# Entry of layer 0's feed-forward: token sums and spread inside the first plain half panel, the third sum ahead of the scaling, the two plain panels in turn

## The chip, the core and the metric

The kernel runs on one core of a Trainium2 chip. The metric is the device time of the whole program, in microseconds (us). The core's engines each take their own instructions in the order in which they were laid down: TensorE (PE) multiplies into PSUM, with its weight loads (PEld) beside it; VectorE (DVE) and ScalarE (ACT) do the elementwise work; GpSimdE (POOL) and SyncE (SP) mostly issue DMAs here.

## The reference, cut to what matters

Two layers of a hybrid backbone over 512 latent tokens and 256 context tokens, 1024 features. The stage around the change is the feed-forward of layer 0, in fp32:

```python
h_lat = h_lat + g_a * o_lat                       # attention's output projection
h_lat = h_lat + g_f * swiglu(modulate(h_lat, sh_f, sc_f), ffn_w_gate_up[l], ffn_w_down[l])
# the same for h_ctx with the context modulation
def rms_norm(x): return x * lax.rsqrt(jnp.mean(x * x, axis=-1, keepdims=True) + EPS)
def modulate(x, shift, scale): return rms_norm(x) * (1 + scale) + shift
def swiglu(h, w_gate_up, w_down):
    g, u = jnp.split(h @ w_gate_up, 2, axis=-1)
    return (jax.nn.silu(g) * u) @ w_down
```

Before the first gate-up product can run, a token's 1024 features must all have their residual, be squared and summed, and the token's features be scaled by the inverse root.

## The kernel before, in words

Features lie on the 128 partitions in 8 tiles (k = 0 to 7), tokens along the free axis: 768 for layer 0, in two halves of 384, TOK1 and TOK2. Every fp32 product is made from three matmuls: each operand is split into a rounded high part (a cast on ACT) and a low part (a subtraction on DVE), and high x high, high x low and low x high are added in PSUM. `parts` (line 1288), `split` (line 340) and `load_w` (line 301) make such splits; `three` (line 757) and `product` (line 1297) issue the matmuls.

`output` (line 1186) makes the attention's output projection with the residual, tile by tile, first for TOK2 and then for TOK1, and beside the TOK1 tiles it normalises TOK2. `Norm.add` squares a residual tile on ACT and adds it to a running sum on DVE (line 355). `Norm.rest` then calls `rstd`: token sums as matmuls with a column of ones (line 365), root on ACT (366), reciprocal on DVE (367), and `spread` (line 449), three transposes of the broadcast column that put the token factors into a PSUM bank. After that `use` of `combined` (line 1246) scales each tile on DVE (line 1235), adds the shift on ACT (line 1236) and splits it. For TOK2 the scaled tiles are called far, for TOK1 near.

The feed-forward's 22 gate-up column blocks (128 columns of the gate and 128 of the up matrix each) come in two kinds. In layer 0 block 0 is done plainly: two panels, gate and up, by the two token halves, four half panels of 24 matmuls (`half` in `first_pairs`). Blocks 1 to 21 are each a `Pair` (line 1306): a scheme with 7 products instead of 8 over the two halves of the features and of the columns, for which sums of the operands are needed: T1 to T4 from the far and near tiles (`sums`, line 1267) and s1 to s4 from the weights (`Pair.weights`, lines 1313 to 1333). Of a pair, `head` needs near operands alone, `body` needs T2, T3 and T1, `tail` needs T4. The head's bank z is copied out (line 1341) before the body adds T2's product to it. The tail of a pair comes after the head of the next.

Modulation vectors still to be made are background steps: `bg(n)` runs n of them. Here two steps of layer 0's last component remain (matmuls of line 191, whose weights lie in the buffers ph and pl, and line 195), then tiles of layer 1 (two DVE products of line 215 each, with the weights in the single buffer rope0).

The order on each engine is set by a planner: it simulates the program and gives an engine the ready instruction that stands first in the code; a buffer is taken when its first writer is placed. `in_order(engine)` (line 630) fixes the order of the instructions in its block on that engine. Buffers that matter: p has 8, ph and pl 4 each, PSUM tags s, t, o, d have 3, 2, 1, 2.

## Time and profile before

| | us |
|---|---|
| median of 3 runs (1613.65, 1618.28, 1618.03) | 1618.03 |
| the profiled execution's own time | 1612.09 |
| its span | 1610.3 |
| PE busy in the span | 1539.6 (96%) |
| DVE busy | 1182.0 (73%) |
| ACT busy | 806.0 (50%) |
| mean granted TensorE clock | 0.986 |

Times inside the profile count from the span's start. A row of the timeline gives start, length, engine, line, operation, output<-inputs, shape and count; in brackets stands how long the engine was idle before it and what ended that. Successive matmuls and elementwise instructions overlap a little, so the cost of one in a row of many is the distance from start to start. A matmul on plain fp32 data (token sums, modulation) is recorded as two passes.

### The profile page before, as it was taken

The numbers are of one execution on the slowest core, as the hardware profiler recorded it, in microseconds if no ns is written. First come the engines' busy times: TensorE is split into PE (matmuls) and PEld (weight loads), VectorE is DVE, ScalarE is ACT, GpSimd is POOL, SyncE is SP. The second block draws the span as 40 slices with busy tenths as digits, with TensorE's granted clock in tenths as the row PEclk, the third lists the DMA queues.
The fourth block names the chain that finished last, engine by engine and source line by source line (L and its number), as shares of the span: only waits on it lengthen the run. The fifth ranks groups of instructions, "written<-read, shape, count | busy, mean of one in ns | idle before, by whom it ended". The sixth has DMA issues, their size and how long they took to land.

```text
span 1610.3 us, 26632 instructions
## 1 busy us (share of the span) xinstructions
PE 1539.6 (96%) x10004; PEld 1375.9 (85%) x10004; DVE 1182.0 (73%) x2367; ACT 806.0 (50%) x1637; POOL 226.7 (14%) x219
## 2 busy tenths in 40 slices
PE   6999989999998999999999998999999999999997
PEld 4686877887988999998989997877889898899996
DVE  5495977577579687785867776768877688687686
ACT  5364587776455333342423244457756554454453
POOL 0152723230000000100000010283003000000000
PEclk9999999999998999999999999999999999999998
DMA  9445342004541465647565766121006133333322
GB/s 341 161 149 190 108 132 80 23 7 159 179 161 59 158 204 169 214 127 246 159 202 196 243 212 210 41 89 66 2 6 200 33 112 124 91 98 118 91 97 84
DMA packets 80465, 214.92 MB, mean 133 GB/s; under 512 B 10192, under 2 KB 17872, under 8 KB 80336
## 3 DMA queue, kind: packets, MB, share of 16 engines
q1 hardware_dynamic: 73552, 188.05, 36.5%
q0 software_dynamic: 4480, 22.02, 3.7%
q10 hardware_dynamic: 2304, 3.15, 0.5%
q8 instruction: 78, 1.28, 0.3%
q14 instruction: 51, 0.42, 0.1%
HBM read 186.97 MB, written 23.07 MB: 130 GB/s over the span
## 4 chain that ended last, share of the span: by engine, by line
PE 73%; DVE 12%; DMA 9%; issue 3%; ACT 2%; POOL 1%; SPq 0%; DVEq 0%; ACTq 0%
PE pso L532 5%; DMA rope<-in_mod_w_dram 4%; PE pss L320 4%; PE pss L321 4%; PE pss L322 4%; PE psd L320 3%; PE psd L321 3%; PE psd L322 3%; PE pss L1302 3%; PE pss L1304 3%; PE pss L1303 3%; PE psd L1304 3%; PE psd L1302 3%; PE psd L1303 3%; PE pst L479 2%
## 5 line engine op out<-in xcount | busy, mean ns | idle before, releaser
L307 ACT CAST wh<-wr 128x512 fp32r<-128x512 f32 (+2 forms) x142 | 108.4, 778 | 202.9 <-PE pss L321 43.3
L308 DVE TENSOR_TENSOR wl<-wr,wh 128x1024 fp32r<-128x1024 f32 (+2 forms) x139 | 127.1, 921 | 78.6 <-ACT wh L307 77.9
L538 ACT ACTIVATE p<-p,sm 128x512 f32<-128x512 f32 (+3 forms) x144 | 105.0, 730 | 26.3 <-DVE sm L542 24.0
L215 DVE CUSTOM_DVE_ANT_0 p<-rope,cond 128x1024 bf16<-128x1024 f32 x64 | 77.0, 1220 | 40.3 <-DMA rope<-in_mod_w_dram 40.1
L321 PE MATMUL psd<-b,wh 128*128 128x256 f32 (+4 forms) x257 | 87.7, 341 | 2.2 <-DVE b L1290 2.2
L1303 PE MATMUL pss<-b,wh 128*128 128x384 f32 (+1 forms) x270 | 84.0, 311 | 1.2 <-DVE b L345 1.2
L1302 PE MATMUL pss<-b,wh 128*128 128x384 f32 (+1 forms) x270 | 84.1, 311 | 0.7 <-ACT b L344 0.7
L1430 POOL DMA_DIRECT2D home<-p x40 | 21.6, 541 | 447.5 <-DVE p L1166 320.5
L1304 PE MATMUL pss<-b,wl 128*128 128x384 f32 (+1 forms) x270 | 83.9, 311 | 0.0
L320 PE MATMUL psd<-b,wh 128*128 128x512 f32 (+4 forms) x217 | 77.8, 358 | 2.1 <-ACT b L430 1.3
L320 PE MATMUL pss<-st,wh 128*128 128x256 f32 (+2 forms) x231 | 78.1, 339 | 0.4 <-ACT wh L307 0.4
L322 PE MATMUL pss<-st,wl 128*128 128x512 f32 (+2 forms) x231 | 77.8, 337 | 0.0
L532 PE MATMUL pso<-ph,b 128*64 128x256 f32 (+1 forms) x384 | 77.3, 359 | 0.3 <-DVE ph L470 0.2
L532 PE MATMUL pso<-pl,b 128*64 128x256 f32 (+1 forms) x384 | 76.8, 359 | 0.7 <-DVE pl L470 0.7
L322 PE MATMUL psd<-b,wl 128*128 128x512 f32 (+4 forms) x217 | 76.0, 351 | 0.0
L1304 PE MATMUL pst<-b,wl 128*128 128x384 f32 (+1 forms) x240 | 74.1, 310 | 0.6 <-DVE wl L1290 0.6
L1302 PE MATMUL pst<-b,wh 128*128 128x384 f32 (+1 forms) x240 | 74.5, 310 | 0.0
L1303 PE MATMUL pst<-b,wh 128*128 128x384 f32 (+1 forms) x240 | 74.5, 310 | 0.0
L321 PE MATMUL pss<-b,wh 128*128 128x256 f32 (+4 forms) x227 | 74.0, 327 | 0.1
L1289 ACT CAST wh<-ph 128x512 fp32r<-128x512 f32 x80 | 46.3, 620 | 43.8 <-PE pst L1303 14.6
L1302 PE MATMUL psd<-b,wh 128*128 128x384 f32 (+1 forms) x210 | 65.8, 313 | 0.0
L1304 PE MATMUL psd<-b,wl 128*128 128x384 f32 (+1 forms) x210 | 65.3, 313 | 0.5 <-DVE wl L1290 0.5
(606 smaller groups left out, 5385.0 us busy)
## 6 DMA issues: line engine op xcount, KB each, us to landing
wr<-in_w_gu_dram SPq DMA_DIRECT2D x88, 512.0 KB, 4.1
rope<-in_mod_w_dram SPq DMA_DIRECT2D x48, 512.0 KB, 3.5
wr<-in_w_out_dram SPq DMA_DIRECT2D x32, 512.0 KB, 3.6
wr<-in_w_dn_dram SPq DMA_DIRECT2D x64, 256.0 KB, 2.8
p<-home SPq DMA_DIRECT2D x40, 384.0 KB, 4.8
home<-p POOLq DMA_DIRECT2D x40, 384.0 KB, 4.5
wr<-in_w_in_dram SPq DMA_DIRECT2D x21, 512.0 KB, 4.0
st<-in_mod_wp_dram SPq DMA_DIRECT2D x32, 256.0 KB, 4.9
```

What stands on the lines that cost most here:

```text
L215: V.tensor_tensor_reduce(out=T("p", [P, D], mybir.dt.bfloat16), in0=w, in1=cond[:, v, :], op0=ALU.mult, op1=ALU.add, scale=1.0, scalar=0.0 ...
L307: S.copy(h, r)
L308: (G if eng else V).tensor_tensor(lo, r, f(h), op=ALU.subtract)
L320: PE.matmul(o, wh[:, k], mh[:, c], start=first and k == 0, stop=False)
L321: PE.matmul(o, wh[:, k], ml[:, c], start=False, stop=False)
L322: PE.matmul(o, wl[:, k], mh[:, c], start=False, stop=last and k == n - 1)
L532: ins = PE.matmul(o[64 * i : 64 * i + 64, c], v(kt), t, start=n == 0, stop=n == len(moving[i]) - 1)
L538: S.activation(p[:, c], p[:, c], AF.Exp, bias=nm, scale=-1.0, accum_out=dn)
L1289: S.copy(h, t)
L1302: PE.matmul(o, wh, xh, start=first and k == 0, stop=False, skip_group_check=not first)
L1303: PE.matmul(o, wh, xl, start=False, stop=False, skip_group_check=not first)
L1304: PE.matmul(o, wl, xh, start=False, stop=k == 3, skip_group_check=not first)
```

## The change

1. `output` gets `hold`. In layer 0's second stream (TOK1) the last tile's square is kept as a second tile, `norm.last`, instead of being added to the running sum, and the normalisation is not run there.
2. `first_pairs` for layer 0: the far half of panel 0 is begun with four of its eight feature tiles (12 matmuls); then the token sums over the two square tiles, root and reciprocal; then `third`, which makes T3 = far's second half minus its first and splits it; then the other 12 matmuls, the spread, and the far half of panel 1. PE's order is fixed over all that.
3. Then the scaling of TOK1 (`norm.use`), and the near halves of both panels in turn, in a fixed order on PE: for each pair of feature tiles the products with the high part of both panels, then the products with the low part of the pair before.
4. `sums` makes T1 and T2 (and T3 in layer 1, where the operands are narrow) of all four tiles first, then T4 in place in the near tiles.
5. The two background steps that stood between the far and near halves are run after the head of pair 1, those after the head of pair 1 after that of pair 2.
6. `token_sums`, `inverse` and `spread_to` are moved or named; the end of layer 0 uses them as before.

```diff
-                norm.add(m, c)
+                if hold and i and m == KT - 1:
+                    norm.last = square_sum(None, norm.src[m], c)
+                else:
+                    norm.add(m, c)
...
+            if hold and i:
+                return
...
+    def token_sums(d, accs, n):
+
+        for i in range(n // P):
+            for j, a in enumerate(accs):
+                PE.matmul(d[:, i : i + 1], a[:, i * P : (i + 1) * P], ones[:, :1], start=j == 0, stop=j == len(accs) - 1)
...
+    def spread_to(col, n):
+
+        o = PS("o")
+        spread(o, [col[:, i : i + 1].to_broadcast([P, P]) for i in range(n // P)])
+        return o
...
+            xs = []
             for i in range(4):
                 tag = "st" if i < 2 else "b"
-                x, y = B(tag="p"), B(tag="p")
...
+                x = B(tag="p")
+                xs.append(x)
...
-                several(x, ("T1", "T2"), tag)
-                V.tensor_tensor(y[:, at1], b22, b12, op=ALU.subtract)
-                V.tensor_tensor(y[:, at2], b21, x[:, at2], op=ALU.subtract)
-                several(y, ("T3", "T4"), tag)
+                several(x, ("T1", "T2", "T3") if narrow else ("T1", "T2"), tag)
+            for i, x in enumerate(xs):
+                tag = "st" if i < 2 else "b"
+                y = near[i][:, at2]
+                V.tensor_tensor(y, y, x[:, at2], op=ALU.subtract)
+                ops["T4"].append(parts(y, *(spare[i] if narrow else (unit(tag), unit(tag)))))
+
+        def third():
+
+            for i in range(4):
+                x = B(tag="p")[:, at1]
+                V.tensor_tensor(x, far[i][:, at2], far[i][:, at1], op=ALU.subtract)
+                ops["T3"].append(parts(x, *(unit("st" if i < 2 else "b") for _ in range(2))))
...
+        if l == 0:
+            with in_order(ON_PE):
+                o = begun(0, 1, order[:4])
+                d = PG()
+                token_sums(d, (norm.acc, norm.last), HT)
+                col = inverse(d, HT)
+                V.reciprocal(col, col)
+                third()
+                begun(0, 1, order[4:], o)
+                r = Columns(spread_to(col, HT), 0)
+                ended(0, 1, o)
+                half(1, 1)
+            for k in order:
+                norm.use(k, r, cs[0], 0)
+            near = [PG()[:, : cs[0].stop] for _ in range(2)]
+            with in_order(ON_PE):
+                for i in range(5):
+                    for o, (h, lo) in zip(near, (ws[0], ws[1])):
+                        for k in (i, i + 4) if i < 4 else ():
+                            x = ops[("11", "21")[k // 4]][i][0]
+                            PE.matmul(o, h[:, k], x, start=k == 0, stop=False)
+                            PE.matmul(o, lo[:, k], x, start=False, stop=False)
+                    for o, (h, _) in zip(near, (ws[0], ws[1])):
+                        for k in (i - 1, i + 3) if i else ():
+                            PE.matmul(o, h[:, k], ops[("11", "21")[k // 4]][i - 1][1], start=False, stop=k == 7)
+            for n in range(2):
+                ended(n, 0, near[n])
+            return [x for x, _ in tiles]
...
-        if l == 0:
-            bg(2)
...
-                    if l == 0 and j == DIRECT[0]:
+                    if l == 0 and j < 3:
                         bg(2)
```

`begun` issues a half panel's matmuls for the feature tiles it is given, `ended` applies Silu or the product with the other panel and splits the result; together they are the former `half`.

More of the change, by code (lines that the diff above doesn't have):

```diff
@@ L1367, in first_pairs, with begun @@
         ws = {}
-        def half(n, second):
+        order = (0, 4, 1, 5, 2, 6, 3, 7)
+        def begun(n, second, ks=order, o=None):
             j, i = panels[n]
@@ L1433, in hybrid_kernel @@
     first_w, banks3 = [], []
-    def token_sums(d, accs, n):
-        for i in range(n // P):
-            for j, a in enumerate(accs):
-                PE.matmul(d[:, i : i + 1], a[:, i * P : (i + 1) * P], ones[:, :1], start=j == 0, stop=j == len(accs) - 1)
-    def inverse(d, n):
-        col = T("sm", [P, 6, 2])[:, : n // P, 0]
-        S.activation(col, d[:, : n // P], AF.Sqrt, bias=eps, scale=1.0 / D)
-        return col
     def final0(src, hs):
```

37 lines of the change are left out of this document (21 added, 16 removed).

## The prediction

> **What bounds the kernel now.** I read the busy time by stage first. Its columns are the stretch, its length, the busy time of PE, PEld, DVE, ACT and POOL with instruction counts, then granted clock, DMA share and GB/s.
>
> ```profile
> 466.78:513.10 46.32, 38.54 (x208) 34.61 (x208) 39.24 (x68) 24.05 (x40) 0.54 (x1) 0.85 0.17 55
> 477.50:487.20 9.70, 4.39 (x30) 2.71 (x29) 8.54 (x20) 8.99 (x17) 0.00 (x0) 0.75 0.21 56
> 487.20:492.70 5.50, 5.49 (x17) 5.49 (x18) 5.50 (x9) 2.58 (x4) 0.00 (x0) 0.51 0.00 0
> 505.60:513.10 7.50, 5.04 (x17) 4.23 (x16) 7.33 (x12) 1.74 (x3) 0.00 (x0) 0.77 0.24 85
> 513.10:560.00 46.90, 46.65 (x266) 44.66 (x266) 30.36 (x54) 17.55 (x34) 0.16 (x1) 1.00 0.45 144
> 560.00:700.00 140.00, 140.00 (x802) 133.21 (x801) 112.31 (x193) 49.80 (x89) 8.49 (x16) 1.00 0.58 189
> 800.00:1003.00 203.00, 193.54 (x1070) 180.79 (x1068) 143.48 (x247) 71.03 (x133) 12.98 (x24) 0.99 0.63 209
> ```
>
> The stretch from 466.78 (first matmul of layer 0's feed-forward) to 513.10 (last product of the body of pair 1) is the only one near the change in which PE is not full: 46.32 - 38.54 = 7.8 us idle, at a mean clock of 0.85. Behind it PE is full for hundreds of us, so a gain won here should reach the end.
>
> Then the order of instructions in that stretch, PE first:
>
> ```profile
> 466.78 0.33 PE L758 MATMUL psd<-st,wh 128*128 128x384 f32 x1
> 470.78 0.33 PE L760 MATMUL psd<-b,wl 128*128 128x384 f32 x1
> 471.04 0.41 PE L191 MATMUL pst<-ph,cond_col 128*32 128x256 f32 x2
> 472.45 0.83 PE L365 MATMUL pss<-ones,p 128*128 128x1 f32 x6
> 473.15 0.42 PE L758 MATMUL pss<-st,wh 128*128 128x384 f32 x1
> 477.26 0.33 PE L760 MATMUL pss<-b,wl 128*128 128x384 f32 x1
> 478.09 0.54 PE L449 MATMUL pso<-ident_r,sm 128*128 128x128 f32 x3
> 483.93 0.69 PE L758 MATMUL pss<-b,wh 128*128 128x384 f32 x1 [1.96 <-ACT b L344]
> 487.21 0.69 PE L759 MATMUL pss<-b,wh 128*128 128x384 f32 x1 [1.64 <-DVE b L345]
> 509.36 0.44 PE L1302 MATMUL pss<-st,wh 128*128 128x384 f32 x1 [0.57 <-ACT p L1348]
> 512.48 0.52 PE L1303 MATMUL pss<-b,wh 128*128 128x384 f32 x1
> 512.80 0.47 PE L1304 MATMUL pss<-b,wl 128*128 128x384 f32 x1
> ```
>
> A plain half is 24 matmuls of 0.174 us ((470.78 - 466.78)/23). The token sums run only at 472.45, behind the first half and modulation matmuls, and the column is spread only at 478.09, behind the second half. DVE waits for exactly that:
>
> ```profile
> 467.89 1.23 DVE L1290 TENSOR_TENSOR wl<-wr,wh 128x1024 fp32r<-128x1024 f32 x1 [0.29 <-ACT wh L1289]
> 469.03 0.55 DVE L355 TENSOR_TENSOR p<-p,p 128x384 f32<-128x384 f32 x1
> 471.75 0.69 DVE L1323 TENSOR_TENSOR pl<-wr 128x512 f32<-128x512 f32 x1 [2.17 <-PE pst L191]
> 474.29 0.17 DVE L367 RECIPROCAL sm<-sm 128x3 f32<-128x3 f32 x1
> 478.66 4.29 DVE L1235 SCALAR_TENSOR_TENSOR p<-b,mod,pso 128x384 f32<-128x384 f32 x8 [4.21 <-PE pso L449]
> 506.02 1.21 DVE L215 CUSTOM_DVE_ANT_0 p<-rope,cond 128x1024 bf16<-128x1024 f32 x1
> 507.16 0.95 DVE L345 TENSOR_TENSOR b<-p,b 128x768 fp32r<-128x768 f32 x1
> 516.79 1.23 DVE L215 CUSTOM_DVE_ANT_0 p<-rope,cond 128x1024 bf16<-128x1024 f32 x1 [3.86 <-DMA rope<-in_mod_w_dram]
> ```
>
> DVE idles 2.17 and 4.21 us and then runs from 478.66 without a gap. The last low part of a T operand ends at 508.11; PE ends the pair's body 5.0 us behind it. In the chain of waits (start, length, what) DVE carries it throughout; one each of a scaling, a subtraction and a 768-wide low part, the length being the time to the next start:
>
> ```profile
> 478.66 0.20 DVE p L1235
> 485.22 0.47 DVE p L1282
> 507.23 0.87 DVE b L345
> ```
>
> So from 478.66 on **DVE sets the end of this stage**; before, the spread's place in PE's order does.
>
> **The change part by part.** First, the token sums. They now come after 12 of the first half's 24 matmuls: 466.78 + 12 x 0.174 = 468.87. Six passes took 473.15 - 472.45 = 0.70 us; with two tiles instead of one they are twelve, 1.4 us, end 470.3. The second tile is the square of the last residual, which ACT has ready in time:
>
> ```profile
> 467.76 0.52 ACT L352 ACTIVATE p<-b 128x384 f32<-128x384 f32 x1
> 473.32 0.26 ACT L366 ACTIVATE sm<-pss,eps 128x3 f32<-128x3 f32 x1 [5.05 <-PE pss L365]
> 478.18 0.62 ACT L1289 CAST ph<-wr 128x512 fp32r<-128x512 f32 x1 [4.59 <-PE psd L191]
> 478.81 1.28 ACT L1378 ACT_TABLE_LOAD   x1
> 480.11 0.49 ACT L1378 ACTIVATE p<-psd 128x384 f32<-128x384 f32 x1
> 481.01 2.14 ACT L1236 ACTIVATE p<-p,mod 128x384 f32<-128x384 f32 x4
> 483.05 0.83 ACT L344 CAST b<-p 128x768 fp32r<-128x768 f32 x1
> 500.86 0.47 ACT L1341 COPY p<-pss 128x384 f32<-128x384 f32 x1
> ```
>
> 467.76 + 0.52 = 468.28, 0.6 us ahead of its use; the DVE addition at 469.03 falls away. Root (0.26) and reciprocal (0.17) with some 0.3 us of hand-over end at 471.0; the other 12 matmuls cover that until 472.4. If the cover went (DVE busy with up to three third sums ahead of the reciprocal) each would cost 0.47 us, and the slack of 1.4 us takes three. The spread (0.5 us) then ends at 472.9: **DVE's scaling starts 478.66 - 472.9 = 5.8 us earlier.**
>
> Second, the third sums move ahead of the scaling. Before, each was a subtraction of 0.47 us and half of a 768-wide low part (T3 and T4 shared it; half of 0.87), inside DVE's closed block: 4 x 0.90 = 3.6 us. Now they are 4 x (0.47 + 0.47) = 3.8 us (384-wide low part, nearest row the 384-wide operations), in the 3.4 us between 469.5 and 472.9 that hold nothing urgent. What leaves the block is 3.6 less an overhang of 0.4: **-3.2 us**. Their four casts ride on ACT, which before sat 5.05 us and then 4.59 us idle there: nothing, as long as the root comes first.
>
> Third, four weight sums of pair 1 (471.75 to 474.3, 4 x 0.6) used that gap before. The third sums take it now, and the modulation matmuls that hold the ph and pl buffers move behind the head of pair 1, so these sums slide into the block: **+2.4 us**. The bounds are 0 (PE runs those matmuls in any idle moment, being ready) and 2.4; I take the upper, since the gap is full.
>
> Fourth, the steps of background modulation move one pair later. The matmuls of line 191 cost PE the same wherever they stand. The two layer-1 tiles (line 215) follow pair 2's head instead of pair 1's, and the first of their four products stood in the block at 506.02: **-1.1 us** if it leaves, 0 if it stays; I take -1.1, since every instruction of pair 2's weights now goes ahead of it.
>
> Fifth, the near halves run in turn and in a fixed order. Per index PE needs 12 x 0.174 = 2.1 us, DVE two scalings of 0.54 and a low part of 0.87 = 1.95, ACT two Identities of 0.53 and a cast of 0.72 to 0.83 = 1.8 to 1.9. PE is the slowest by a little; the second far half (24 x 0.174 = 4.2) keeps it at work until 477.1, while ACT gives the first high parts at 472.4 + 1.28 + 0.49 + 2 x 0.53 + 0.83 = 476.1. So the run starts without a wait and costs nothing by itself. But the lead is 1 us, and other casts and sums share both engines' queues, which run in order: I put **+1.0** on DVE's block for waits on ACT, between 0 and 2.3 (a third cast or two in between each time).
>
> Sixth, T4 goes behind all the other sums: the same DVE work, ahead of pair 1's weights either way: 0, and up to -3.6 if it goes behind them.
>
> The sum for the last operand of pair 1's body: -5.8 - 3.2 + 2.4 - 1.1 + 1.0 = -6.7, so 508.1 becomes 501.4. PE runs out of near and head matmuls at about 477.1 + 8.4 + 4.2 = 489.7, or 492 with the modulation matmuls, and then takes T operands as they come. It will be cold again as it was at 509.36 (12 matmuls, 0.32 us apart, in 512.80 + 0.32 - 509.36 = 3.8 us instead of 2.1), so I leave the 5.0 us between last operand and last product as they are: 506.4 instead of 513.1. Of that, DVE's earlier end is kept for the following pairs, since PE is 99% full from there. **Gain 6.7 us.** In the profiled execution (span 1610.3, its own time 1612.09) that is 1605.4; against the median of the runs, 1618.03, **1611.3**. The profiled execution lies 6 us under that median, as the fastest run (1613.65) lies 4 us under it, so chance among runs is as large as what I look for.
>
> One rule speaks on the cold clock. By the Trainium skill, page "TensorE: Matmul & The Clock Gate", section "HAM oscillation — how this bites in real kernels", PE drops to half clock only when it idles more than about 3.4 us. Here the clock fell to half at 509.36 after waits of which none was over 1.2 us (7.50 - 5.04 = 2.5 us in all within that stretch), and by 487.2 after waits under 2 us: the trace does not bear the rule out as a limit for single gaps. By the rule the new body would run at full clock after short gaps, which would give some 1.7 us more (1609.6, an estimate); the sum keeps the trace's price.
>
> **The rivals.** *PE becomes the bound.* With all of DVE's deferrable work (T4, the layer-1 products, next pair's sums) behind the operands, PE sees no gap: 46.32 us less 7.8 idle, less the half-clock loss (17 matmuls at 487.2, four from 483.93 and 12 at 509.36, each 0.32 - 0.174 = 0.146: 4.8), plus 0.7 for the doubled token sums: 34.4 us, end 501.2, gain 11.9, **1606.1**. For it: the rows per index above balance, and PE has 12 us of loss to give. Against it: DVE's continuous work.
>
> *The queue takes it back.* The layer-1 products keep their place, and because the first now runs earlier than the second tile can be loaded, DVE waits for the DMA in front of pair 1's remaining weights as it did at 516.79: 6.7 - 1.1 - 3.86 = 1.7 gained, **1616.3**. For it: that wait stood in the chain already, after a product which had been ready long before. Against it: these products now rank behind pair 2's weights.
>
> *The change loses: p buffers.* Eight exist. The four near tiles now live until T4 and the four x tiles too, so pair 1's s and t get none until T4 begins, and the copy of z (line 1341, at 500.86 before) must precede T2, T3 and T1. If T4 stands last: operands 501.4, T4's first part 0.94 + a cast 0.5, copy 0.5, body 36 matmuls (the first 12 cold: 3.8 + 4.2) and 0.6 for the second copy: 511.9, no gain; and if the two layer-1 products and their DMA wait stand ahead of T4 too (1.1 + 1.1 + 3.9): 518.0, **1622.9**. It decides once z's copy comes later than about 504. For it: the count of tiles. Against it: nothing else of DVE's is as urgent by then, and T4 ranks before the weights.
>
> That the change doesn't do what it says is open only for the order outside the two fixed runs, where a planner decides again, also for the chunk boundaries behind 800 (203.0 - 193.54 = 9.5 us of idle PE, which may move by a few us either way).
>
> **How the numbers follow.** A measurement of this kernel can tell about 0.3%, 4.9 us, from no change. Forecast 0.47, with a range of its own of 1608 to 1615; PE-bound 0.23; taken back 0.22; p buffers 0.08. Of the forecast's 0.47 I count 0.05 as under 4.9 us. Faster is 0.42 + 0.23 = 0.65, same 0.05 + 0.22 = 0.27, slower 0.08. The range reaches from 1605 (PE-bound, with a us for chance) to 1617 (taken back, likewise), and leaves out the last rival.
>
> **What would show it.** The 12-pass token sums before 470.5 and a spread near 472.5; first scaling near 473; the four third sums ahead of it; near matmuls at 0.174 us from about 477, without waits over 1 us; the layer-1 products after 510; the body's last product of pair 1 near 506. It would be wrong if ACT's first high parts came after 478 (the fixed run then stands still and goes cold), if DVE shows gaps over 2 us before 500, if z's copy of pair 1 comes after 504, or if the stretch ends earlier and the chunk boundaries behind it lose the same.

## The result, and the profile after

The changed kernel takes 1607.57 us (median of 5 runs, 1605.55 to 1609.28), the kernel before 1618.03 in the runs beside it. The ratio is 0.9942, with a 95% interval of 0.9927 to 0.9957: 9.4 us gained by the ratio, 10.5 by the medians. Measured a second time beside other runs of the kernel before, it came to 0.9936 (0.9919 to 0.9952). The forecast was 6.7 us gained and 1611.3; the range of 1605 to 1617 holds the time, which lies 0.4 us under the 1608 to 1615 that the forecast had by itself.

The profiled execution of the changed kernel has a span of 1603.8 us. In it PE comes to layer 0's feed-forward at 468.29, and before at 466.78, although PE's order and its idle time ahead of it (29.9 us) are the same; over the profiles of this document that moment lies between 466.75 and 471.22. So 1.5 us are chance among executions, and I measure from the first far matmul of the stage. I call the stretch from there to the first residual addition of the down projection *the stage*; it holds the same work in both kernels but for six more passes of token sums. The windows of it, first before, then after (columns as in the prediction: stretch, length, then busy time of PE, PEld, DVE, ACT, POOL, and clock, DMA share, GB/s):

```profile
466.78:557.16 90.38, 82.35 (x459) 76.92 (x459) 67.14 (x118) 40.20 (x71) 0.54 (x1) 0.92 0.30 98
```

```profile
468.29:507.60 39.31, 38.37 (x237) 34.37 (x237) 38.13 (x71) 27.16 (x49) 0.54 (x1) 1.00 0.36 122
468.29:547.09 78.80, 77.86 (x465) 72.68 (x465) 65.58 (x120) 40.55 (x75) 0.54 (x1) 1.00 0.41 139
```

The stage is 11.6 us shorter. PE's idle time falls from 90.38 - 82.35 = 8.0 us to 0.9, which is 7.1 of them; PE's busy time falls by 4.5, though it has more matmuls, because the clock is whole (1.00 instead of 0.92). The first row of after ends with the last product of pair 1's body, 39.31 us behind the start. By then the whole head of pair 2 is done too (24 matmuls). Before, T1's product ended at 513.10, 46.32 us behind the start, with four of these 24 done. But that wasn't the end of the body: the product of T3 still lacked two matmuls, for which an operand came late (DVE's row first, then PE's):

```profile
511.98 0.94 DVE L345 TENSOR_TENSOR b<-p,b 128x768 fp32r<-128x768 f32 x1
516.59 0.34 PE L1303 MATMUL pss<-b,wh 128*128 128x384 f32 x1
516.76 0.34 PE L1304 MATMUL pss<-b,wl 128*128 128x384 f32 x1
```

So body and head 2 were both done at 516.9 before, 50.1 us behind the start, and at 507.5 after, 39.2 behind it: for the same products that is 10.9 us sooner. What is left in this stage for PE to lose is 0.9 us.

The order on PE in the timeline of after (start, busy time, engine, line, operation, out<-in, shape, count, and in brackets the idle time before it with its releaser):

```profile
468.29 0.33 PE L758 MATMUL pss<-st,wh 128*128 128x384 f32 x1
470.36 1.40 PE L1218 MATMUL psd<-ones,p 128*128 128x1 f32 x12
474.10 0.51 PE L449 MATMUL pso<-ident_r,sm 128*128 128x128 f32 x3
478.65 0.34 PE L1443 MATMUL pst<-b,wh 128*128 128x384 f32 x1
480.03 0.34 PE L1332 MATMUL psd<-b,wh 128*128 128x384 f32 x1
480.48 0.41 PE L191 MATMUL pss<-ph,cond_col 128*32 128x256 f32 x2
494.89 0.44 PE L1332 MATMUL psd<-st,wh 128*128 128x384 f32 x1 [0.80 <-ACT p L1371]
507.36 0.33 PE L1334 MATMUL psd<-b,wl 128*128 128x384 f32 x1
```

The twelve passes stand amid the first far half, the spread behind it, and the near run (lines 1443 to 1447) is threaded with head products (1332) and modulation matmuls (191), which fill the moments in which an operand isn't there. The wait of 0.80 us for z's copy is the only long one of the stage. DVE in the same view:

```profile
467.10 0.69 DVE L1353 TENSOR_TENSOR pl<-wr 128x512 f32<-128x512 f32 x1 [0.17 <-DMA wr<-in_w_gu_dram]
471.30 0.69 DVE L1320 TENSOR_TENSOR pl<-wr,ph 128x512 fp32r<-128x512 f32 x1
471.91 1.96 DVE L1313 TENSOR_TENSOR p<-b 128x384 f32<-128x384 f32 x4
473.78 0.17 DVE L1429 RECIPROCAL sm<-sm 128x3 f32<-128x3 f32 x1
473.87 1.00 DVE L1320 TENSOR_TENSOR st<-p,st 128x384 fp32r<-128x384 f32 x2
475.25 2.18 DVE L1258 SCALAR_TENSOR_TENSOR p<-b,mod,pso 128x384 f32<-128x384 f32 x4
487.14 1.01 DVE L1306 TENSOR_TENSOR p<-p,p 128x384 f32<-128x384 f32 x2
489.82 0.55 DVE L1306 TENSOR_TENSOR p<-p,p 128x384 f32<-128x384 f32 x1
492.09 0.55 DVE L1298 TENSOR_TENSOR p<-b,p 128x384 f32<-128x384 f32 x1
499.04 0.95 DVE L345 TENSOR_TENSOR b<-p,b 128x768 fp32r<-128x768 f32 x1
500.99 0.23 DVE L199 SCALAR_TENSOR_TENSOR mod<-pst,modb 128x2 f32<-128x2 f32 x2 [0.39 <-PE pst L195]
507.25 1.22 DVE L215 CUSTOM_DVE_ANT_0 p<-rope,cond 128x1024 bf16<-128x1024 f32 x1
```

From 467.10 on DVE has no gap until 500.99. Pair 1's weight sums (from 467.10, the last low part at 471.30) are out of the way before the third subtractions (471.91), the reciprocal stands behind all four of these, and the scaling begins at 475.25. Three of the four T4 subtractions (line 1306) run ahead of the last tile's T1 sum (line 1298, 492.09). The low part at 499.04 is the last one that the body of pair 1 needs. ACT:

```profile
471.80 0.27 ACT L1223 ACTIVATE sm<-psd,eps 128x3 f32<-128x3 f32 x1 [1.49 <-PE psd L1218]
477.65 0.82 ACT L344 CAST b<-p 128x768 fp32r<-128x768 f32 x1
494.36 0.48 ACT L1371 COPY p<-psd 128x384 f32<-128x384 f32 x1
```

The first high part (477.65 + 0.82) is there just before the near run begins at 478.65; z of pair 1 is copied at 494.36 (500.86 before).

The second profile of the same kernel shows how much of this is chance:

```profile
468.49:548.13 79.64, 78.02 (x465) 72.79 (x465) 66.42 (x121) 40.67 (x75) 0.54 (x1) 1.00 0.40 137
```

79.6 us instead of 78.8, with 1.6 us idle. The gain of the stage is thus 10.7 to 11.6 us by these two against the one profile of the kernel before; the median times have 9.4 to 10.5 at the end of the kernel. In the profiles, counted from the first far matmul, 8.0 of 11.6 us are left at the end and 9.2 of 10.7: 3.5 and 1.6 go back, in the first pair about one each among layer 0's chunk boundaries, around layer 1's first pairs and behind these.

### The profile page after: what moved, and what is told of

It is laid out like the page before. It is cut to its first block, busy times and chain, and to the rows that moved or that the text cites. A ratio compares the mean times of both kernels' runs of the same rounds, so it can differ in the third digit from the quotient of the medians.

```text
span 1603.8 us, 26659 instructions
## 1 busy us (share of the span) xinstructions
PE 1537.6 (96%) x10010; PEld 1373.2 (86%) x10010; DVE 1180.7 (74%) x2370; ACT 807.3 (50%) x1641; POOL 226.7 (14%) x219
## 3 DMA queue, kind: packets, MB, share of 16 engines
q10 hardware_dynamic: 2304, 3.15, 0.5%
## 4 chain that ended last, share of the span: by engine, by line
PE 75%; DVE 9%; DMA 8%; issue 3%; ACT 2%; POOL 2%; SPq 0%; DVEq 0%; ACTq 0%; POOLq 0%
PE pso L532 5%; PE pss L320 4%; PE pss L321 4%; PE pss L322 4%; DMA rope<-in_mod_w_dram 3%; PE psd L320 3%; PE psd L321 3%; PE psd L322 3%; PE pss L1334 3%; PE pss L1332 3%; PE pss L1333 3%; PE psd L1332 3%; PE psd L1334 3%; PE psd L1333 3%; PE pst L1334 2%
## 5 line engine op out<-in xcount | busy, mean ns | idle before, releaser
L1334 PE MATMUL pss<-b,wl 128*128 128x256 f32 (+1 forms) x258 | 79.5, 308 | 0.9 <-DVE wl L1320 0.8
L1333 PE MATMUL pss<-b,wh 128*128 128x256 f32 (+1 forms) x258 | 79.4, 308 | 0.0
L1332 PE MATMUL pss<-b,wh 128*128 128x256 f32 (+1 forms) x258 | 79.1, 306 | 0.0
L1333 PE MATMUL psd<-b,wh 128*128 128x384 f32 (+1 forms) x222 | 70.1, 316 | 0.0
L1332 PE MATMUL psd<-b,wh 128*128 128x384 f32 (+1 forms) x222 | 69.9, 315 | 0.0
L1334 PE MATMUL psd<-b,wl 128*128 128x384 f32 (+1 forms) x222 | 69.6, 315 | 0.0
```

Source lines behind the costliest of these rows:

```text
L1332: PE.matmul(o, wh, xh, start=first and k == 0, stop=False, skip_group_check=not first)
L1333: PE.matmul(o, wh, xl, start=False, stop=False, skip_group_check=not first)
L1334: PE.matmul(o, wl, xh, start=False, stop=k == 3, skip_group_check=not first)
```

## The experiments

Two theories were set against each other. *Theory 1* is the prediction's own: DVE's chain sets the end of the stage, and each part of the change gives its microseconds, to be added. *Theory 2*: after the change PE sets it, and the change is worth what it takes away of PE's idle time and half clock; the parts aren't additive. Each kernel is the changed one with the edit shown. All are profiled and timed beside the kernel before; the stage is measured as above, idle is its length less PE's busy time.

| kernel | stage, us | PE idle | PE busy | ratio to before (95%) |
|---|---|---|---|---|
| before | 90.38 | 8.0 | 82.35 | 1 |
| the change | 78.80 | 0.9 | 77.86 | 0.9942 (0.9927 to 0.9957) |
| the change, again | 79.64 | 1.6 | 78.02 | 0.9936 (0.9919 to 0.9952) |
| sums late | 86.93 | 6.6 | 80.38 | 0.9961 (0.9945 to 0.9977) |
| third sums late | 83.38 | 2.5 | 80.85 | 0.9947 (0.9928 to 0.9966) |
| near halves apart | 82.24 | 3.4 | 78.83 | 0.9955 (0.9934 to 0.9977) |
| modulation back | 82.15 | 4.1 | 78.06 | 0.9965 (0.9944 to 0.9986) |
| sums alone | 86.03 | 4.7 | 81.38 | 0.9954 (0.9939 to 0.9970) |
| T4 each | 81.68 | 2.3 | 79.40 | 0.9938 (0.9913 to 0.9963) |
| more sums | 84.07 | 3.7 | 80.36 | 0.9969 (0.9955 to 0.9982) |
| more ahead | 85.01 | 4.6 | 80.43 | 0.9968 (0.9952 to 0.9984) |
| more sums, modulation later | 86.00 | 5.4 | 80.62 | 1.0000 (0.9984 to 1.0017) |
| layer 1 likewise | 78.91 | 1.1 | 77.85 | 0.9923 (0.9904 to 0.9942) |
| layer 1, scaling first | 80.03 | 2.0 | 78.00 | 0.9908 (0.9888 to 0.9927) |

### Each part left out

**Sums late**: token sums, spread and scaling as before, the third sums still ahead.

```diff
-    output(..., norm, BG[2], hold=True)
+    output(..., norm, BG[2])
...
-                o = begun(0, 1, order[:4])
-                d = PG()
-                token_sums(d, (norm.acc, norm.last), HT)
-                col = inverse(d, HT)
-                V.reciprocal(col, col)
...
-                begun(0, 1, order[4:], o)
-                r = Columns(spread_to(col, HT), 0)
-                ended(0, 1, o)
+                half(0, 1)
...
-            for k in order:
-                norm.use(k, r, cs[0], 0)
```

> The changed kernel, but the token sums, the spread and the scaling of TOK1 stand in the code where they stood before (ahead of the far halves, without a fixed place among them); the third sums ahead of the far halves, the near panels in turn, the later background steps stay. Measure: the stage from the first far matmul to the first residual of the down projection, 557.15 - 466.78 = 90.4 us in the kernel before and 547.09 - 468.29 = 78.8 us in the changed one. Theory 1 (the prediction's: VectorE's chain sets the stage, each part of the change is worth its own term): the scaling starts up to 5.8 us later, the stage takes 84 to 85 us, the clock stays full. Theory 2 (TensorE sets the stage; the change is worth what idle time and half clock it takes away, and parts are not additive): the delay of the scaling opens a gap of 3 us or more ahead of the near run, the clock falls, and the stage takes 85 to 88 us with a window at a clock of 0.5.

**Third sums late**: the T3 sums go back behind T1 and T2, into DVE's block.

```diff
                 several(x, ("T1", "T2", "T3") if narrow else ("T1", "T2"), tag)
+            if not narrow:
+                third()
             for i, x in enumerate(xs):
...
-                third()
```

> The changed kernel, but the third sums T3 stand behind T1 and T2 again (still split by themselves, 384 wide). Theory 1: VectorE gets 3.2 us more to do between the scaling and the last operand of pair 1's body, the stage takes 81 to 82.5 us. Theory 2: TensorE has the near run and the heads to do meanwhile, so VectorE's 3.2 us are mostly hidden: 78.8 to 80 us, at full clock.

**Near halves apart**: one after the other, PE's order left to the planner.

```diff
-            near = [PG()[:, : cs[0].stop] for _ in range(2)]
-            with in_order(ON_PE):
...
             for n in range(2):
-                ended(n, 0, near[n])
+                half(n, 0)
```

> The changed kernel, but the near halves of the two plain panels one after the other, in the planner's order, instead of in turn in a fixed order. Theory 1: VectorE's work is the same, 78.8 to 79.5 us. Theory 2: the first panel alone asks for an index every 1.05 us while VectorE and ScalarE need 1.9 us for one, so TensorE idles up to 0.85 us at each of the first indices unless other products fill in, and may go cold: 80 to 83 us.

**Modulation back**: the background steps where they were.

```diff
+            bg(2)
             near = [PG()[:, : cs[0].stop] for _ in range(2)]
...
-                    if l == 0 and j < 3:
+                    if l == 0 and j == DIRECT[0]:
```

> The changed kernel, but the background steps stand where they stood (two between far and near halves, two behind the head of pair 1). Theory 1: the modulation weights take the ph and pl buffers ahead of pair 1's weight sums, whose 2.4 us slide into VectorE's block, and one layer-1 product (1.1 us) comes back into it: 81 to 82.5 us. Theory 2: TensorE still has enough to do, and the steps are the same work wherever they stand: 78.8 to 80 us.

Leaving a part out lengthened the stage by 8.1, 4.6, 3.4 and 3.4 us: 19.5 in all, where all four together give 11.6 (against the second profile, 7.3, 3.7, 2.6 and 2.5: 16.1 of 10.7). As measured the parts don't add. Of the forecasts, late sums (86.9) and near halves apart (82.2) came inside theory 2's range, modulation back (82.2) inside theory 1's, and third sums late (83.4) above both. Where PE stood is in the waits of the timeline, the rows of each kernel in the order above:

```profile
480.90 0.66 PE L1434 MATMUL pst<-b,wh 128*128 128x384 f32 x1 [2.78 <-ACT b L344]
489.30 0.62 PE L191 MATMUL pss<-ph,cond_col 128*32 128x256 f32 x4 [0.97 <-DMA ph<-in_mod_wp_dram]
501.07 0.74 PE L191 MATMUL pss<-pl,cond_col 128*32 128x256 f32 x4 [2.18 <-DMA pl<-in_mod_wp_dram]
```

```profile
492.72 0.44 PE L1334 MATMUL pss<-st,wh 128*128 128x384 f32 x1 [1.09 <-ACT st L1321]
494.37 0.62 PE L191 MATMUL pss<-ph,cond_col 128*32 128x256 f32 x4 [1.21 <-DMA ph<-in_mod_wp_dram]
```

```profile
482.60 1.07 PE L191 MATMUL pss<-ph,cond_col 128*32 128x256 f32 x4 [2.83 <-DMA ph<-in_mod_wp_dram]
```

```profile
498.70 0.44 PE L1332 MATMUL psd<-b,wh 128*128 128x384 f32 x1 [1.37 <-ACT wh L1319]
```

With late sums the near run waits 2.78 us for its first high part, and with the third sums late PE waits 1.09 us for a high part of such a sum: theory 1's price. But in these two and with the near halves apart, PE also stands before matmuls of line 191 that wait for a *load* (3.15, 1.21 and 2.83 us): the planner, with a different set of ready work, put these background matmuls ahead of products on PE's in-order queue, and the weights in ph or pl came later than it had counted. Nobody needs them so soon. Half clock stands behind these waits in all three. What a part left out costs is thus set partly by where the filler lands: 7.2 of the 19.5 us are such waits, the half clock behind them not counted. So these runs don't show whether the parts would add with the filler out of the way. The kernel with modulation back has no wait for a load: its waits, for high parts of pair weights and a copy of z, all from ACT, are 0.5 to 1.4 us each, 4.1 us in all, and its clock stays whole. In the whole runs the four lie at 0.9947 to 0.9965, all above the change's 0.9942, with intervals that overlap its own: the times alone don't rank the parts, the stage does.

### One part alone

Only the token sums and the spread amid the first far half are kept. The four sums of `sums` are again as in the kernel before (T3 and T4 together), and the background steps stand where they were.

```diff
...
-                third()
...
-            near = [PG()[:, : cs[0].stop] for _ in range(2)]
...
+            bg(2)
             for n in range(2):
-                ended(n, 0, near[n])
+                half(n, 0)
...
-                    if l == 0 and j < 3:
+                    if l == 0 and j == DIRECT[0]:
```

> Only the first part of the change: token sums and spread amid the first far half. Third sums, T4 order, near halves and background modulation stand as in the kernel before. Theory 1 (terms add): the scaling starts 5 to 5.8 us sooner than before and every operand with it; leaving this part out cost 8.1 us, so alone it should bring about that, the stage 82 to 85 us against 90.4 before. Theory 2 (what counts is that PE has no gap): with the third sums in the block again and the near halves in the planner's order PE is starved later on, as in the kernels that left these parts out; the stage takes 85 to 89 us, with 5 us or more of idle and half clock.

It took 86.0 us: 4.4 gained, short of theory 1's 5 to 8, inside theory 2's range. The timeline of PE shows why:

```profile
471.19 0.38 PE L1218 MATMUL psd<-ones,p 128*128 128x1 f32 x2
472.92 1.28 PE L1218 MATMUL psd<-ones,p 128*128 128x1 f32 x10
477.33 0.54 PE L449 MATMUL pso<-ident_r,sm 128*128 128x128 f32 x3
```

Two of the twelve passes run, then modulation matmuls take PE until 472.92, then the other ten. A fixed order holds among its own instructions; the planner may still put others in between. With the background steps in their old place the spread comes 8.9 us behind the first far matmul (477.33 - 468.47), in the change 5.8. So the fourth part, of which the prediction said that its matmuls cost PE the same wherever they stand, is a condition of the first: it keeps them out of the token sums. The kernel with modulation back has the same spread at 8.9.

### T4 in its own tiles

```diff
-            xs = []
...
-                xs.append(x)
...
-            for i, x in enumerate(xs):
-                tag = "st" if i < 2 else "b"
-                y = near[i][:, at2]
-                V.tensor_tensor(y, y, x[:, at2], op=ALU.subtract)
+                y = B(tag="p")[:, at1]
+                V.tensor_tensor(y, near[i][:, at2], x[:, at2], op=ALU.subtract)
                 ops["T4"].append(parts(y, *(spare[i] if narrow else (unit(tag), unit(tag)))))
```

> Each T4 sum in a p tile of its own right behind its T1 and T2, instead of in place behind all of them. This undoes the last part of the change, which I had put at nothing. Theory 1: four subtractions and low parts (4 x 0.94 us) come ahead of later T1 and T2 operands on DVE, which the planner may order otherwise: the stage 0 to 3.8 us longer, 78.8 to 82.6. Theory 2: T4 has 12 us and more to spare, PE waits for nothing that stands behind it: at most 1 us, 79.8. In both the p buffers are short: if z's copy of pair 1 (26.07 us behind the first far matmul in the changed kernel) comes over 3 us later, it is the tiles, not DVE's time.

The stage took 81.7 us, 2.0 to 2.9 longer: inside theory 1's wide range, above theory 2's. z's copy of pair 1 came 28.59 us behind the first far matmul instead of 26.07 or 26.92, so under the 3 us that would have spoken for a shortage of p tiles. Again the one long wait is the filler's, with half clock behind it, in the timeline of PE:

```profile
498.00 1.07 PE L191 MATMUL pss<-pl,cond_col 128*32 128x256 f32 x4 [2.28 <-DMA pl<-in_mod_wp_dram]
```

So what T4's place costs by itself isn't shown. The whole run can't be told from the change (0.9938).

### More work on DVE

Does DVE have slack now? **More sums** computes the eight T1 and T2 sums twice; **more ahead** computes the four third subtractions three times, in front of the scaling. Each is eight subtractions of 0.47 us more.

```diff
-                V.tensor_tensor(x[:, at1], b12, b11, op=ALU.subtract)
-                V.tensor_tensor(x[:, at2], b22, x[:, at1], op=ALU.subtract)
+                for _ in range(1 if narrow else 2):
+                    V.tensor_tensor(x[:, at1], b12, b11, op=ALU.subtract)
+                    V.tensor_tensor(x[:, at2], b22, x[:, at1], op=ALU.subtract)
```

> This kernel computes the eight first and second sums of layer 0's T operands of pair 1 twice: eight more DVE subtractions of 0.47 us, 3.8 us more inside DVE's closed block, ahead of the operands of the body of pair 1. The output is the same. Theory 1 (DVE's chain sets the end of the entry, terms add): the last operand, the body of pair 1 and the stage from the first far matmul to the first down projection come 3.3 to 3.8 us later than the changed kernel's 78.8 us, so 82 to 82.6, and the ratio to before rises by 0.002 to about 0.9965. Theory 2 (after the change PE sets the end, with DVE ahead of it by some us): PE has the head of pair 2 and modulation matmuls to put in place of the late operands; the stage grows by under 1.5 us, to 80.3 at most, and the ratio stays at 0.994 to 0.995.

```diff
-                V.tensor_tensor(x, far[i][:, at2], far[i][:, at1], op=ALU.subtract)
+                for _ in range(3):
+                    V.tensor_tensor(x, far[i][:, at2], far[i][:, at1], op=ALU.subtract)
```

> This kernel computes the four third subtractions three times: eight more DVE subtractions of 0.47 us, 3.8 us, ahead of the reciprocal and so of the scaling. The output is the same. Theory 1: the scaling starts 3.8 us later (10.8 us behind the first far matmul instead of 7.0), and so do all operands; the stage takes 82.6 us. Theory 2: the near matmuls start late by up to 3.8 us, and PE fills only part of that with head and modulation matmuls: the stage grows by what PE idles or runs at half clock and by no more, between 1 and 3 us, to 80 to 82 us. A growth of 3.8 us or more with idle PE of 4 us would be theory 1's price at the front, and together with a small growth in the kernel with more sums in the block it would place the limit at the start of the scaling and not along the block.

The stage grew by 4.4 to 5.3 us and by 5.4 to 6.2: more than the 3.8 us added, and more than either theory gave. The waits of PE in the first, then in the second:

```profile
497.88 1.07 PE L191 MATMUL pss<-ph,cond_col 128*32 128x256 f32 x4 [2.67 <-DMA ph<-in_mod_wp_dram]
```

```profile
482.63 0.69 PE L1444 MATMUL pst<-b,wh 128*128 128x384 f32 x1 [3.34 <-ACT b L344]
```

In the second the scaling starts only 1.1 us later (+8.08 instead of +6.97), because the last tile's subtractions and most of the third sums' casts went behind the first six scalings. There the casts stand on ACT ahead of the first high part, and the near run waits 3.34 us for it: with 4.6 us idle in all, 0.92 of them before a load, this is theory 1's price at the front, as its expectation put it. In the first, operands were waited for by 0.6 us at most; it is the load again, and the half clock behind it. So whether DVE's time itself cost anything was open there. The third kernel of this set is *more sums* with the background steps two pairs later, out of the way:

```diff
-                    if l == 0 and j < 3:
+                    if l == 0 and 2 < j < 5:
```

> The kernel with eight sums computed twice (3.8 us more DVE work ahead of the T operands of pair 1), and the two background modulation steps of this stage moved two pairs later. In the kernel with the doubled sums alone the only long wait of PE was not for an operand but for a load of modulation weights (2.67 us), and half clock came behind it, so whether DVE's 3.8 us themselves cost anything stayed open. Theory 1 (DVE's chain sets the end): PE waits at the T products for DVE's low parts or ACT's copies, 3 us or more in all before the body of pair 1 ends, and goes to half clock there; the stage takes 82 to 84 us. Theory 2 (PE sets it, DVE has slack): with no load to wait for, PE's waits stay under 1.5 us in all and the clock whole; 16 to 24 modulation matmuls fewer stand in the stage, so it takes 77 to 80 us.

```profile
483.34 0.62 PE L1448 MATMUL pst<-b,wh 128*128 128x384 f32 x2 [1.17 <-DVE b L345]
493.91 0.44 PE L1333 MATMUL pss<-st,wh 128*128 128x384 f32 x1 [0.82 <-ACT wh L1320]
496.73 0.44 PE L1333 MATMUL psd<-b,wh 128*128 128x384 f32 x1 [2.20 <-ACT wh L1320]
506.66 0.44 PE L1334 MATMUL psd<-b,wh 128*128 128x384 f32 x1 [0.42 <-DVE b L345]
490.14 1.57 ACT L344 CAST st<-p 128x768 fp32r<-128x768 f32 x2 [6.28 <-DVE p L1300]
```

Now PE waits 4.6 us in the four PE rows, with half clock behind the third: theory 1's forecast for this kernel (3 us or more, and half clock), and its stage of 86.0 is beyond the 82 to 84 given. Two of the waits are for DVE's low parts. The two in the middle are for high parts of pair weights, which ACT casts behind those of the T operands, and before these it had waited 6.28 us for DVE's doubled sums (last row). So theory 2's slack of DVE, 3.8 us or more, doesn't show. How much of the 86.0 belongs to the moved filler and how much to the sums isn't separated, since the change with the filler moved and no more sums wasn't run. The whole run has none of the gain left (1.0000), though the stage has 4.4 us of it; where the rest goes wasn't followed.

Taken together: both engines are at their limit in the changed kernel. PE has 0.9 to 2.0 us left, and no run shows slack in DVE's chain. My sum looked at one of them, theory 2 at the other.

### The same in layer 1

In layer 1 the changed kernel still does it the old way, and its PE timeline has the gaps that layer 0 had:

```profile
1246.35 0.39 PE L758 MATMUL pss<-b,wh 128*128 128x256 f32 x1 [2.82 <-ACT b L344]
1247.78 0.58 PE L759 MATMUL pss<-b,wh 128*128 128x256 f32 x1 [0.81 <-DVE b L345]
```

**Layer 1 likewise** holds back the last square there too (`hold=True`) and puts token sums and spread amid its first far half:

```diff
-        for n in range(min(3, len(panels))):
-            half(n, 1)
+        n1 = cs[0].stop
+        with in_order(ON_PE):
+            o = begun(0, 1, order[:4])
+            d = PG()
+            token_sums(d, (norm.acc, norm.last), n1)
+            col = inverse(d, n1)
+            V.reciprocal(col, col)
+            begun(0, 1, order[4:], o)
+            r = Columns(spread_to(col, n1), 0)
+            ended(0, 1, o)
+            half(1, 1)
+            half(2, 1)
+        for k in order:
+            norm.use(k, r, cs[0], 0)
```

> The changed kernel, and in layer 1 too the token sums and the spread stand amid the first far half, with the sum of squares of the last residual held back for PE as in layer 0. In the kernel before, PE idles some 3.6 us at layer 1's entry and runs 3.4 us at half clock (17 gained at most 1.7). Both theories: the scaling of layer 1 starts 2 to 4 us sooner. Theory 1: DVE's chain is shorter by that, and the rest of the kernel ends 2 to 4 us sooner: about 1604.5 us median, 0.992 of before. Theory 2: only what PE idles and loses to the half clock can be won, at most 5.3 us: 1602 to 1606; less where the gap moves behind the near halves, since the third sums stay in DVE's block there.

The spread came 4.00 us behind layer 1's first far matmul, but the scaling only at 8.55 (9.38 in the changed kernel, so 0.8 sooner where 2 to 4 were expected), and PE still had a gap of 2.23 us. Its DVE timeline names the reason:

```profile
1239.17 0.42 DVE L1417 TENSOR_TENSOR p<-p,psd 128x256 f32<-128x256 f32 x1 [4.18 <-PE psd L760]
1240.41 3.22 DVE L1258 SCALAR_TENSOR_TENSOR p<-b,mod,pso 128x256 f32<-128x256 f32 x8
```

The Silu product of the second panel stands ahead of the scaling in the code and therefore on DVE, and waits 4.18 us for PE's matmuls, with the scaling, ready since the spread, behind it. So the **scaling first** version issues it ahead of those products:

```diff
-            half(1, 1)
-            half(2, 1)
+            o1, o2 = begun(1, 1), begun(2, 1)
         for k in order:
             norm.use(k, r, cs[0], 0)
+        ended(1, 1, o1)
+        ended(2, 1, o2)
```

> The changed kernel with layer 1's token sums and spread amid its first far half, and the scaling issued ahead of the Silu products of the second and third panel's far halves, which in the first version of this edit stood ahead of the scaling on DVE and waited 4.18 us for PE there (scaling 8.55 us behind layer 1's first far matmul although the spread came at 4.00; 9.38 in the changed kernel). Both theories: scaling near 4.6 us behind the first far matmul, near matmuls without a gap behind the third far half. Theory 1 (DVE's chain): layer 1's first pairs come 4.8 us sooner. Theory 2 (PE's gaps and half clock): what there is to win is 2.82 + 0.81 us idle and some 1.7 us of half clock, 5.3 us less 0.5 for the doubled token sums. Both give about 1602.8 us, a ratio of 0.991 to 0.992; if the planner behind it gives some back, 1605.

```profile
1241.75 3.22 DVE L1258 SCALAR_TENSOR_TENSOR p<-b,mod,pso 128x256 f32<-128x256 f32 x8 [1.36 <-PE pso L449]
```

The scaling starts 4.49 us behind the first far matmul. The windows of the first 30 us of layer 1's feed-forward, the changed kernel and then this one:

```profile
1234.19:1264.19 30.00, 26.37 (x209) 25.93 (x208) 15.23 (x29) 14.59 (x29) 0.74 (x1) 0.94 0.22 67
```

```profile
1237.26:1267.26 30.00, 29.89 (x254) 29.81 (x253) 19.50 (x41) 15.13 (x32) 0.75 (x1) 1.00 0.24 74
```

PE is idle for 0.1 us instead of 3.6, at whole clock, and does 45 more matmuls in the same 30 us. Layer 1's pairs come 4.8 us sooner by the milestones of the two traces, and 4.5 of it are left at the end. The time is 1601.93 us median (1596.85 to 1604.14), ratio 0.9908 (0.9888 to 0.9927). The changed kernel on the same chip gave 1604.98 and 0.9936. The intervals overlap, so the times alone don't tell the two apart; the traces show the gap gone that the edit was made for, and of all that ran this version has the lowest median.

The changed kernel itself, again:

> The changed kernel itself once more, beside the kernel before and the two others. Expected: a ratio to before of 0.993 to 0.996; the stage from the first far matmul to the first down projection 78.8 us to within 0.3, since the order of all instructions is the same. What differs between two executions is then the chance among runs, for which I expect 1 to 3 us at the first far matmul.

The ratio was as expected; the stage differed by 0.84 us where I had given 0.3. DVE's timeline of this second profile has the cause:

```profile
468.15 0.69 DVE L1353 TENSOR_TENSOR pl<-wr 128x512 f32<-128x512 f32 x1 [1.01 <-DMA wr<-in_w_gu_dram]
470.08 0.61 DVE L1166 SCALAR_TENSOR_TENSOR b<-pst,mod,b 128x384 f32<-128x384 f32 x1
```

Pair 1's weight sums now stand ahead of the attention's last residual addition (line 1166) on DVE, and they wait for their load, here 1.01 us instead of 0.17. The last square, the token sums and the scaling come 0.8 us later for it. So the sums that left the closed block brought a small dependence on a load with them.

Four profiles have this stage with the same order on PE, DVE and ACT, since the two layer-1 kernels leave it as it is. They differ in that one wait:

| profile | DVE's wait for the load, us | scaling behind the first far matmul | stage |
|---|---|---|---|
| the change | 0.17 | 6.97 | 78.80 |
| layer 1 likewise | 0.29 | 7.08 | 78.91 |
| the change, again | 1.01 | 7.80 | 79.64 |
| layer 1, scaling first | 1.43 | 8.22 | 80.03 |

The scaling starts 1.26 us later from first to last, and the stage takes 1.23 us more, at whole clock and with no wait for filler. So at its front the changed kernel has no slack: DVE's delay reaches PE in full, which waits for the last square and for the spread amid its fixed order. The gain of the stage is 10.3 to 11.6 us over the four.

## Why the prediction was right, and where it was not

The direction and the place were right: the profile after shows the entry of layer 0's feed-forward shortened, and the time is inside the range. It came out 3.7 us under the forecast, and by its amount it is the rival *PE becomes the bound* (11.9 us): 10.7 to 11.6 in the stage. By the prediction's own steps, measured from the first far matmul:

- **Scaling 5.8 us earlier.** 11.89 became 6.97 (second profile 7.80): 4.9 us, 4.1 in the second. The token sums came as I said; but the reciprocal went behind all four third subtractions, where I had given the slack for three, and three low parts came ahead of the scaling too, which I had put into the gap and not before the scaling. So this term was too large by 0.9.
- **Third sums leave the block, -3.2.** They do: all four subtractions stand at 471.91. Putting them back cost 3.7 to 4.6 us, but of that PE waited only 1.09 us for such an operand; 1.21 are a load wait, and PE's busy time is 3.0 higher, with 6.8 us at half clock behind the two. So the size of this term isn't shown.
- **Weight sums slide in, +2.4.** This term failed. I said that the modulation matmuls behind head 1 would hold ph and pl, and that the gap was full. But by moving the background steps the change frees these buffers *earlier*: the sums ran at 467.10 to 472.0, before the third sums. Worth 0, the lower end of the bounds, as long as their load is there.
- **Waits on ACT, +1.0.** 0: DVE has no gap to 500.99.
- **Layer-1 product leaves, -1.1.** It does, as said, though at 507.25, ahead of the 510 that I gave as a sign.
- **T4 behind the sums, 0.** The order doesn't hold for the last tile: three T4 subtractions and two of their low parts stand ahead of its T1 sum, and so of the last operand. At 0.47 us each that is some 2.3 us, an estimate, where the sum has nothing. A shortage of p tiles would do that (the plain panels' Silu tile, four near tiles and three x tiles are eight), but no run tests it.
- **The last operand** then ends at 499.04 + 0.95 = 499.99, 31.7 us behind the start, where my sum gave 34.6. For before I took 508.11, 41.3 us behind the start, the end of T1's and T2's last low part. That was a misreading: the low part of 511.98 holds T3 and T4 of the last tile, which the body needs too, and ends 46.1 us behind the start.
- **5.0 us kept to the last product, with a cold clock.** This is the step that failed most. It took 7.5 us, to 507.5, so that the body ended 39.2 us behind the start, near the 39.6 that I gave, by errors against each other: that is luck. In those 7.5 us PE wasn't waiting: it did head 2. I had counted a gain at one milestone, T1's last product at 513.10, which wasn't even the end of the body: with the last of T3 the body ended at 516.9, and 20 matmuls of head 2 (3.5 us) stood in between. From end to end, with head 2 done in both, the gain is 10.9 us. I had also kept the half clock, which goes (PE's busy time in the stage is 4.5 us lower). What counts for a stage behind which PE is full is PE's idle time and clock over the whole of it, not the date of one product.
- **Rivals.** The p buffers: z's copy at 494.36, ten us short of where it would decide. Taken back: about 1 us of 10.7 to 11.6 by the medians, 1.6 to 3.5 in the profiles, and not by the queue that I named. PE as the bound: the amount is right, its reason only half; I said against it that DVE's work is continuous, which is true, and both hold.

Of the signs listed, the token sums before 470.5 (they begin at 470.36), the near run without waits over 1 us, the four third sums ahead of the scaling and z's copy came as said. The spread at 474.10 against 472.5, the scaling at 475.25 against 473 and the near run at 478.65 against 477 are 1.5 us of chance at the entry and up to 0.8 of real delay. The products of line 215 came at 507.25 and not after 510.

## What to carry to other kernels

Where a stage with idle PE is followed by one in which PE is full, sum PE's idle time and half clock over the whole stage, and let that be the ceiling; a sum along the other engine's chain tells whether one gets there, and the two must be made together. A milestone for such a sum must have the same work done before and after. Work that fills gaps (the next pair's head, background steps) counts as part of the change when it is moved, for it can clear the path of what is urgent, as it did with the token sums here, or stand in an in-order queue before a load that nobody needs yet. And a reduction that ends in a scaling can be put amid the first independent matmuls, if what the same engine has to do for these stands behind the scaling in its queue: in layer 1 that order alone was the difference between 8.55 and 4.49 us.

## What the runs showed of the hardware

One wait sets PE back twice. In the kernel with more sums PE was idle for 2.67 us and then ran at half clock for 6.1 us (windows):

```profile
495.21:497.88 2.67, 0.00 (x1) 0.00 (x1) 2.67 (x6) 2.67 (x6) 0.00 (x0) 0.90 0.61 188
497.88:504.00 6.12, 6.12 (x22) 4.87 (x23) 6.12 (x12) 2.63 (x7) 0.00 (x0) 0.50 0.02 5
```

Matmuls of 384 columns were 0.32 us apart there instead of 0.174. In layer 1 of the changed kernel the half clock came about 1.2 us after the gap of 2.82 us, with a second wait of 0.81 us in between, and lasted 3.4 us (matmuls of 256 columns 0.21 us apart instead of 0.12). But 4.1 us of idle time in shorter pieces can cost no clock at all, as the kernel with modulation back shows, whose longest wait was 1.37 us:

```profile
495.00:515.00 20.00, 15.91 (x86) 14.62 (x85) 19.46 (x35) 11.42 (x22) 0.00 (x0) 1.00 0.29 93
```

The Trainium skill, page "TensorE: Matmul & The Clock Gate", section "HAM oscillation — how this bites in real kernels", puts the limit at idle gaps of more than some 3.4 us. Here single gaps of 2.18 to 2.83 us were enough in several kernels. In the kernel before it was a cluster of waits under 2 us, and in the one with third sums late two waits of 1.09 and 1.21 us within 3 us, with 6.8 us at a clock of 0.50 behind them. Where page and measurement differ, the measurement decides. Whether one gap has a fixed limit between 1.4 and 2.2 us, and what a cluster adds, these runs don't settle.
